# A row's sum of ReLU on one core: the first columns of the split row move to VectorE, and the last sum's two waits change places

## The chip, the cores and the metric

The kernel runs on one core of a Trainium2 chip. The metric is device time in microseconds (us). VectorE is DVE in the profile, ScalarE is ACT, SyncE is SP; DVEq and SPq are the sequencers of VectorE and SyncE. A *stamp* is a time read from the trace to the nanosecond, where the views of the profile round to hundredths of a microsecond. A *semaphore* is a counter that the program has an engine or a transfer raise (`then_inc`) and another wait for (`wait_op`, `wait_ge`). "Lands" means that the last of the sixteen semaphore updates arrives that the trace has for each load (in the kernel before, 154.913 to 155.398 for the load with rows 0 and 1). A sum is recorded as two instructions, the clamping and summing one and one that the trace calls the read of its *accumulator* (0.08 us on VectorE, 0.19 on ScalarE); the semaphore comes after that read (in the kernel before, VectorE's read of the first piece's sum ends at 157.721 and its semaphore comes at 157.732). "e1" to "e10" are the experiments.

## The reference, cut to what matters

```python
# x: (32, 512, 1024) float32, 64 MiB
relu_x = np.maximum(x, 0)
return np.sum(relu_x, axis=-1).astype(np.float32)
```

16,384 rows of 1024 columns, each clamped at zero and summed. On 128 partitions that is 128 rows a partition.

## The kernel before

The first 112 rows of every partition come in blocks of 16: mostly ScalarE clamps, VectorE sums. The last 16 come in loads of 8 and 4 rows, then the last four in a special cut. Of those four, rows 0, 1 and 3 are summed whole by ScalarE, VectorE and ScalarE. Row 2 is the **split row**: it is cut into four column ranges that arrive in four loads, so that little work is left behind the last byte. Each range is clamped and summed by itself. The last operation finds the other partial sums as extra columns behind its own data and adds them in (they are not negative, so the clamp doesn't change them).

```python
TAIL = [8, 4]
ACT_PIECE, END_PIECE = 340, 240     # first and last range of the split row
PIECES = [220, 224]                 # the two ranges between, which arrive last
...
def dve_row(ap, accum_out, loaded):          # VectorE: clamp and sum, one instruction
    i = nc.vector.tensor_scalar(out=ap, in0=ap, scalar1=0.0, scalar2=None,
                                op0=MAX, op1=ADD, accum_out=accum_out)
    if loaded is not None:
        i.wait_op(loaded, 16, "sem-ge")      # the wait is the instruction's own
    i.then_inc(sems.dve, 1)
...
loaded = load(flat[:, at : at + b], src[:, :b])          # rows 0, 1, first range of row 2
act_row(buf[:, c, :], res[:, m : m + 1], loaded)         # ScalarE: row 0
sums_act = n_act
act_row(flat[:, at + split : at + b], others[0], None)   # ScalarE: first range
piece_act = n_act
dve_row(buf[:, c + 1, :], res[:, m + 1 : m + 2], loaded) # VectorE: row 1
sums_dve = n_dve
loaded = load(flat[:, at + end : at + 4 * D], src[:, end:])  # last range of row 2, row 3
act_row(buf[:, c + 3, :], res[:, m + 3 : m + 4], loaded)     # ScalarE: row 3
dve_row(flat[:, at + end : at + 3 * D], others[1], loaded)   # VectorE: last range
... # loads of the two pieces; stores of the sums that are complete
for i in range(len(PIECES) - 1):
    dve_row(parts[i][:, :], others[2 + i], arrived[i])       # VectorE: first piece
nc.vector.wait_ge(sems.act, piece_act)
nc.vector.wait_ge(sems.dve, n_dve)
nc.vector.tensor_scalar(... last piece and the other sums ...,
    accum_out=res[:, NT - 2 : NT - 1],
).wait_op(arrived[-1], 16, "sem-ge").then_inc(sems.dve, 1)
n_dve += 1
store(NT - 2, 2, n_act, n_dve)     # SyncE waits for ScalarE, then for VectorE, and stores
```

Below, the load with the last range of row 2 and with row 3 is called the **second load**, the two pieces the **first** and the **last piece**.

Of the kernel before, what the change touches and what calls it, by code (L numbers as in the profile page):

```python
# [9 lines left out]
ROWS = 16  # L10
# [7 lines left out]


TAIL = [8, 4]  # L20
ACT_PIECE, END_PIECE = 340, 240
PIECES = [220, 224]

EARLY = 1

# [1 line left out]
def kernel(tc: tile.TileContext, x: bass.AP, out: bass.AP):  # L27
    nc = tc.nc
    sems = Semaphores(tc)

    tc.close()
    tc.compile()
    nc.cur_bb = nc.bb_map[tc.start_bb_name]
    body = nc.cur_bb.bb.instructions
    ends = list(body)
    body.clear()
    n_stores = relu_sum(nc, sems, x, out)
    body.extend(ends)


    nc.cur_bb = nc.bb_map[tc.start_bb_name + "_end"]
    nc.cur_bb.bb.instructions.clear()
    nums = sorted(s.num for s in (*sems.loads, sems.act, sems.dve))
    cleared = range(nums[0], nums[-1] + 1)
    assert len(cleared) == len(nums)
    nc.sync.sem_clear(cleared)
    nc.sync.wait_ge(sems.stored, 16 * n_stores).then_inc(sems.stored, -16 * n_stores)
    open_without_barrier(tc, EARLY)


class Semaphores:
    def __init__(self, tc: tile.TileContext):
        n = len(TWO) + len(TAIL) + 2 + len(PIECES)
        self.loads = [tc.alloc_semaphore(f"load{i}") for i in range(n)]
        self.act = tc.alloc_semaphore("act")
        self.dve = tc.alloc_semaphore("dve")
        self.stored = tc.alloc_semaphore("stored")


def relu_sum(nc, sems: Semaphores, x: bass.AP, out: bass.AP):  # L60
    x_flat = x.flatten_outer_dims()
    N, D = x_flat.shape
    NT = N // P
    NB = len(TWO)
    assert N == P * NT == P * ROWS * (NB + 1)
    assert sum(TAIL) == ROWS - 4 and ACT_PIECE + END_PIECE + sum(PIECES) == D

    bufs = [nc.alloc_sbuf_tensor(f"io{i}", [P, ROWS, D], F32) for i in range(NBUF)]
    res = nc.alloc_sbuf_tensor("res", [P, NT], F32)

    extra = len(PIECES) + 1
    parts = [
        nc.alloc_sbuf_tensor(f"piece{i}", [P, w + extra * (i + 1 == len(PIECES))], F32)
        for i, w in enumerate(PIECES)
    ]
# [21 lines left out]
    def load(dst, src, after=None):  # L97
        nonlocal n_load
        dma = nc.sync.dma_start(out=dst, in_=src)  # L99
        if after:  # L100
            dma.wait_op(sems.dve, after[1], "sem-ge")
        dma.then_inc(sems.loads[n_load], 16)
        n_load += 1
        return sems.loads[n_load - 1]
# [25 lines left out]
    def act_row(ap, accum_out, loaded):  # L130
        nonlocal n_act
        i = nc.scalar.activation(out=ap, in_=ap, func=RELU, accum_out=accum_out)  # L132
        if loaded is not None:
            i.wait_op(loaded, 16, "sem-ge")
        i.then_inc(sems.act, 1)
        n_act += 1

    def dve_row(ap, accum_out, loaded):
        nonlocal n_dve
        i = nc.vector.tensor_scalar(  # L140
            out=ap,
            in0=ap,
            scalar1=0.0,
            scalar2=None,
            op0=MAX,
            op1=ADD,
            accum_out=accum_out,
        )
        if loaded is not None:
            i.wait_op(loaded, 16, "sem-ge")  # L150
        i.then_inc(sems.dve, 1)
        n_dve += 1
# [40 lines left out]
    flat = buf[:, :, :].rearrange("p c d -> p (c d)")  # L193
    src = rows(m, 4).rearrange("p c d -> p (c d)")
    at = c * D
    split = 2 * D
    b = split + ACT_PIECE
    end = split + D - END_PIECE
    last, w = parts[-1], PIECES[-1]
    others = [last[:, w + i : w + i + 1] for i in range(extra)]  # L200
    loaded = load(flat[:, at : at + b], src[:, :b])
    act_row(buf[:, c, :], res[:, m : m + 1], loaded)
    sums_act = n_act
    act_row(flat[:, at + split : at + b], others[0], None)
    piece_act = n_act
    dve_row(buf[:, c + 1, :], res[:, m + 1 : m + 2], loaded)
    sums_dve = n_dve
    loaded = load(flat[:, at + end : at + 4 * D], src[:, end:])
    act_row(buf[:, c + 3, :], res[:, m + 3 : m + 4], loaded)
    dve_row(flat[:, at + end : at + 3 * D], others[1], loaded)  # L210
    arrived = []
# [9 lines left out]

    for i in range(len(PIECES) - 1):
        dve_row(parts[i][:, :], others[2 + i], arrived[i])
    nc.vector.wait_ge(sems.act, piece_act)
    nc.vector.wait_ge(sems.dve, n_dve)  # L225
    nc.vector.tensor_scalar(  # L226
        out=last[:, :],
        in0=last[:, :],
# [2 lines left out]
        op0=MAX,  # L231
        op1=ADD,
        accum_out=res[:, NT - 2 : NT - 1],
    ).wait_op(arrived[-1], 16, "sem-ge").then_inc(sems.dve, 1)
    n_dve += 1
    store(NT - 2, 2, n_act, n_dve)
    return n_store
# [49 lines left out]
```

## Time and profile before

| | before |
|---|---|
| median of three runs | 161.2 us (161.14 to 161.52) |
| span of the profiled run | 159.7 us |
| VectorE, ScalarE busy | 117.2 us (73%), 104.7 us (66%) |
| input moved | 67.11 MB at 421 GB/s, so 159.4 us |
| last piece lands (stamp) | 157.566 us |
| last store issued (stamp) | 158.306 us |

The table is read from its last rows. The input takes the whole span up to 157.57 (the packets take 98.0% of 16 engines' span by the page). What this change works on is the 0.74 us from there to the issue of the last store. From that issue to the end of the span are 1.426 us (stamps).

### The profile page before, as it was taken

What the parts mean: (1) busy time and instruction counts of PE and PEld (TensorE: products, weight loads), DVE (VectorE), ACT (ScalarE), POOL (GpSimd) and SP (SyncE); (2) the same over time, 40 slices, a digit from 0 to 9 for tenths busy, and PEclk for the clock granted to TensorE, in tenths of its full rate; (3) what the DMA queues carried; (4) which work ended last, traced back from release to release, by engine and by line L of the source; (5) the groups of instructions that cost most, each with busy time, mean ns of one, the idle gap of its engine ahead of it and who ended that gap; (6) DMA issues with size and microseconds to landing.
All of it is one profiled execution on the core that took longest, in us unless ns stands there. A gap on an engine that the chain in (4) does not pass through costs nothing.

```text
span 159.7 us, 120 instructions
## 1 busy us (share of the span) xinstructions
DVE 117.2 (73%) x41; ACT 104.7 (66%) x52; POOL 0.2 (0%) x4
## 2 busy tenths in 40 slices
DVE  0000000009999499994999999999999999999985
ACT  3000059990699708996099941999339992499996
POOL 0000000000000000000000000000000000000000
DMA  7996996996997999979979969969969969898993
GB/s 263 525 525 263 525 525 263 525 492 295 525 460 328 525 394 394 525 345 443 525 328 460 525 279 509 525 263 525 525 263 525 492 295 525 345 443 386 414 417 113
DMA packets 2304, 67.18 MB, mean 421 GB/s; under 512 B 640, under 2 KB 896, under 8 KB 1024
## 3 DMA queue, kind: packets, MB, share of 16 engines
q1 hardware_dynamic: 2304, 67.18, 98.0%
HBM read 67.11 MB, written 0.07 MB: 421 GB/s over the span
## 4 chain that ended last, share of the span: by engine, by line
DMA 44%; DVE 33%; ACT 17%; another core or an unknown queue 3%; SPq 1%; issue 0%; DVEq 0%
DMA io<-in_x_dram 44%; DVE res L125 32%; ACT io L117 17%; SPq L99 1%; DVE io L140 0%; DVE piece L226 0%; DVE piece L140 0%; DVEq L225 0%
## 5 line engine op out<-in xcount | busy, mean ns | idle before, releaser
L125 DVE TENSOR_REDUCE res<-io 128x8 f32<-128x8192 f32 (+2 forms) x9 | 101.1, 11287 | 40.0 <-ACT io L117 40.0
L117 ACT ACTIVATE io<-io 128x8192 f32<-128x8192 f32 (+2 forms) x9 | 81.7, 9110 | 47.7 <-DMA io<-in_x_dram 47.7
L132 ACT ACTIVATE io<-io 128x1024 f32<-128x1024 f32 (+1 forms) x21 | 21.3, 1017 | 5.7 <-DMA io<-in_x_dram 5.7
L140 DVE TENSOR_SCALAR_CACHE_REDUCE io<-io 128x1024 f32<-128x1024 f32 (+1 forms) x14 | 15.5, 1157 | 0.9 <-DMA io<-in_x_dram 0.9
L132 ACT ACTIVATION_READ_ACCUMULATOR io<-io 128x1 f32 x21 | 3.9, 187 | 0.0
L117 ACT ACT_TABLE_LOAD x1 | 1.3, 1283 | 0.1
L140 DVE DVE_READ_ACCUMULATOR io<-io 128x1 f32 x14 | 1.2, 82 | 0.0
L226 DVE TENSOR_SCALAR_CACHE_REDUCE piece<-piece 128x227 f32<-128x227 f32 x1 | 0.4, 390 | 0.2 <-DVE piece L140 0.2
L140 DVE TENSOR_SCALAR_CACHE_REDUCE piece<-piece 128x220 f32<-128x220 f32 x1 | 0.4, 378 | 0.0
L271 POOL MEMSET const-bfloat16-1.0<- 128x1 bf16 x1 | 0.1, 102 | 0.0
L271 POOL MEMSET const-uint8-127<- 128x1 uint8 x1 | 0.1, 102 | 0.0
L271 POOL MEMSET const-float32-0.0<- 128x1 f32 x1 | 0.1, 99 | 0.2 <-issue 0.2
L271 POOL MEMSET const-float32-1.0<- 128x1 f32 x1 | 0.1, 99 | 0.0
L140 DVE DVE_READ_ACCUMULATOR piece<-piece 128x1 f32 x1 | 0.1, 85 | 0.0
L226 DVE DVE_READ_ACCUMULATOR piece<-piece 128x1 f32 x1 | 0.1, 83 | 0.0
## 6 DMA issues: line engine op xcount, KB each, us to landing
io<-in_x_dram SPq DMA_DIRECT2D x1, 4096.0 KB, 21.6
io<-in_x_dram SPq DMA_DIRECT2D x1, 2048.0 KB, 26.1
io<-in_x_dram SPq DMA_DIRECT2D x1, 1194.0 KB, 28.5
io<-in_x_dram SPq DMA_DIRECT2D x1, 632.0 KB, 29.6
io<-in_x_dram SPq DMA_DIRECT2D x7, 26.9
piece<-in_x_dram SPq DMA_DIRECT2D x1, 112.0 KB, 29.2
piece<-in_x_dram SPq DMA_DIRECT2D x1, 110.0 KB, 29.4
out_dram<-res SPq DMA_DIRECT2D x1, 55.0 KB, 1.6
```

Of the source, the lines that this page charges most:

```text
L99: dma = nc.sync.dma_start(out=dst, in_=src)
L117: i = nc.scalar.activation(out=ap, in_=ap, func=RELU)
L125: nc.vector.tensor_reduce(out=res[:, m : m + n], in_=ap, axis=mybir.AxisListType.X, op=ADD).wait_op(sems.act, n_act, "sem-ge").then_inc(se ...
L132: i = nc.scalar.activation(out=ap, in_=ap, func=RELU, accum_out=accum_out)
L140: i = nc.vector.tensor_scalar(out=ap, in0=ap, scalar1=0.0, scalar2=None, op0=MAX, op1=ADD, accum_out=accum_out,)
L226: nc.vector.tensor_scalar(out=last[:, :], in0=last[:, :], scalar1=0.0, scalar2=None, op0=MAX, op1=ADD, accum_out=res[:, NT - 2 : NT - 1],) ...
L271: nc = _bacc.Bacc("TRN2", target_bir_lowering=False, num_devices=1)
```

## The change

Its intent: ScalarE is relieved of the first range, which VectorE sums in time in which it waits for the second load. The last operation then needs nothing of ScalarE. Its one remaining wait for other sums becomes its own, and the wait for its load, expected to be met earlier, stands ahead as an instruction. The cut is moved with it.

```diff
-ACT_PIECE, END_PIECE = 340, 240
-PIECES = [220, 224]
+START_PIECE, END_PIECE = 280, 260
+PIECES = [240, 244]
...
-    act_row(flat[:, at + split : at + b], others[0], None)
-    piece_act = n_act
     dve_row(buf[:, c + 1, :], res[:, m + 1 : m + 2], loaded)
     sums_dve = n_dve
+    dve_row(flat[:, at + split : at + b], others[0], None)
...
-    nc.vector.wait_ge(sems.act, piece_act)
-    nc.vector.wait_ge(sems.dve, n_dve)
+    nc.vector.wait_ge(arrived[-1], 16)
     nc.vector.tensor_scalar(
...
-    ).wait_op(arrived[-1], 16, "sem-ge").then_inc(sems.dve, 1)
+    ).wait_op(sems.dve, n_dve, "sem-ge").then_inc(sems.dve, 1)
```

More of the change, by code (lines that the diff above doesn't have):

```diff
@@ L65, in relu_sum @@
     assert N == P * NT == P * ROWS * (NB + 1)
-    assert sum(TAIL) == ROWS - 4 and ACT_PIECE + END_PIECE + sum(PIECES) == D
+    assert sum(TAIL) == ROWS - 4 and START_PIECE + END_PIECE + sum(PIECES) == D
     bufs = [nc.alloc_sbuf_tensor(f"io{i}", [P, ROWS, D], F32) for i in range(NBUF)]
@@ L196, in relu_sum @@
     split = 2 * D
-    b = split + ACT_PIECE
+    b = split + START_PIECE
     end = split + D - END_PIECE
```

## The prediction

> **What bounds the kernel now.** I read the page first, for the engine shares and the DMA row:
>
> ```profile
> DVE 117.2 (73%) x41; ACT 104.7 (66%) x52; POOL 0.2 (0%) x4
> ...
> HBM read 67.11 MB, written 0.07 MB: 421 GB/s over the span
> ```
>
> No compute engine is full. The transfers are: 67.11 MB at 421 GB/s is 159.4 us of a span of 159.7. The change moves no byte more or less, so the body of the kernel can't change. What is left is the end, where the input has landed and the last sums are still to be made and stored. So second I read the chain of waits, its last part in order of time (start, duration, what):
>
> ```profile
> 127.39 29.59 DMA io<-in_x_dram
> 156.98 0.02 issue
> 157.01 0.41 DVE io L140 x2
> 157.42 0.32 DVE piece L140 x2
> 157.73 0.03 issue
> 157.76 0.05 DVEq L225
> 157.81 0.07 issue
> 157.88 0.40 DVE piece L226 x2
> ```
>
> The end is set by VectorE: three sums after the load that lands at 156.98 (240, 220 and 224+3 columns), and between the second and the third a wait that is an instruction of its own (DVEq L225). Third, the timeline of the last 5 us (start, duration, engine, line, operation), to see which engines have room there:
>
> ```profile
> 155.42 1.22 DVE L140 TENSOR_SCALAR_CACHE_REDUCE io<-io 128x1024 f32<-128x1024 f32 x1 [0.51 <-DMA io<-in_x_dram]
> 156.38 0.19 ACT L132 ACTIVATION_READ_ACCUMULATOR io<-io 128x1 f32 x1
> 156.47 0.47 ACT L132 ACTIVATE io<-io 128x340 f32<-128x340 f32 x1
> 156.57 0.08 DVE L140 DVE_READ_ACCUMULATOR io<-io 128x1 f32 x1
> ...
> 157.00 1.06 ACT L132 ACTIVATE io<-io 128x1024 f32<-128x1024 f32 x1
> 157.01 0.40 DVE L140 TENSOR_SCALAR_CACHE_REDUCE io<-io 128x240 f32<-128x240 f32 x1 [0.36 <-DMA io<-in_x_dram]
> 157.33 0.08 DVE L140 DVE_READ_ACCUMULATOR io<-io 128x1 f32 x1
> 157.33 0.38 DVE L140 TENSOR_SCALAR_CACHE_REDUCE piece<-piece 128x220 f32<-128x220 f32 x1
> 157.64 0.09 DVE L140 DVE_READ_ACCUMULATOR piece<-piece 128x1 f32 x1
> 157.88 0.39 DVE L226 TENSOR_SCALAR_CACHE_REDUCE piece<-piece 128x227 f32<-128x227 f32 x1 [0.16 <-DVE piece L140]
> 157.97 0.19 ACT L132 ACTIVATION_READ_ACCUMULATOR io<-io 128x1 f32 x1
> 158.20 0.08 DVE L226 DVE_READ_ACCUMULATOR piece<-piece 128x1 f32 x1
> ```
>
> VectorE sits idle for 0.36 us before 157.01: that is where the added sum will go. It is idle again for 0.16 us before 157.88: that is the wait's cost. ScalarE's last sum ends at 157.97 + 0.19 = 158.16, VectorE's at 158.28. The last store needs both, so ScalarE is only 0.12 us behind: more than that the change can't gain by speeding VectorE alone. The last store is issued at 158.31 (stamp of the trace), takes 1.4 us to land (DMA issues of the page), and that ends the span.
>
> When do the four last loads land? Issue start plus issue-to-landing gives 126.89 + 28.5 = 155.39 (rows 0, 1 and the first 340 columns of row 2), 127.39 + 29.6 = 156.99 (the end of row 2 and row 3), 127.87 + 29.4 = 157.27 (220 columns), 128.37 + 29.2 = 157.57 (224 columns). Row 2 is the split row. The third sum at 157.88 therefore waits for no load: its data had been there for 0.31 us.
>
> [...] L225 is such a one, 50 ns busy on VectorE's sequencer, and from the second sum's semaphore at 157.73 to the third sum's start at 157.88 pass 0.15 us. Where an instruction carries the wait itself, as the 1024-column sum at 155.42 does, start follows the last landing update (stamp 155.398) by 0.02 us. [...] with a sum taken along, start to start is 1.15 us for 1024 columns and 0.32 us for 240, so 1.05 ns a column[...]; I cost columns at 1.05 ns. [...]
>
> **The change, part by part.**
>
> Loads. Columns of the split row go from 340 | 220 | 224 | 240 to 280 | 240 | 244 | 260. The first load shrinks by 60 columns (1194 to 1164 KB), the second grows by 20 (632 to 642), the pieces by 20 each (110 and 112 to 120 and 122). The sum is the same and so is the last landing, 157.57. Between the landings at 155.40 and 156.98, 632 KB took 1.58 us, that is 2.5 ns per KB. The first load lands 30 KB earlier, 0.07 us: 155.32. The second lands 20 KB earlier, 0.05 us: 156.93. The first piece 10 KB earlier: 157.25.
>
> ScalarE loses the 340-column sum, 0.47 + 0.19 us less some overlap. It lay between 156.47 and 157.04, and the row-3 sum behind it starts 0.02 us after its load. So this frees ScalarE but moves its end only with the load: 158.16 - 0.05 = 158.11. Off the path: worth nothing by itself.
>
> VectorE gains a 280-column sum. Start to start: 0.33 for 240 columns plus 40 x 1.05 ns = 0.37 us. It begins when the 1024-column sum gives way, 155.34 + 1.15 = 156.49, and is over at 156.86, before the load at 156.93. It fits into the idle time with 0.07 us to spare. Cost on the path: nothing.
>
> VectorE's sums after that load: 260 columns 0.35, 240 columns 0.33, from 156.95: the second gives way at 157.63, its accumulator read ends 0.085 us later and the semaphore comes at about 157.73. That is the same stamp as before: 0.05 us earlier start, 40 columns (0.04 us) more.
>
> The wait. Before: semaphore 157.73, sequencer wait, third sum at 157.88. After: the load's wait stands ahead as its own instruction and is met at 157.57, so it is done by about 157.57 + 0.02 + 0.05 = 157.64, and the sum can be in place by 157.71 (0.07 us from the end of the sequencer's wait to the start is what the old one took). The sum's own wait then fires 0.02 us after 157.73: start 157.75. **Saved: 0.13 us.** The last sum has 247 columns for 227: 0.02 us back.
>
> Sum at the end: 0.01 earlier semaphore or none, -0.13, +0.02: VectorE's last semaphore moves from 158.29 to about 158.18. ScalarE, at 158.11 to 158.12, stays just behind. The store is the same 1 KB. So the time falls by **about 0.1 us**, from 161.2 to 161.1, 0.07%.
>
> **Rivals.**
>
> *The wait is only exchanged.* If the separate wait on the load holds the sequencer so that the last sum is pushed late, part of the 0.13 us stays. For it: the margin above is only 0.02 to 0.04 us (157.71 against 157.75). Against it: the load lands 0.16 us before the other sum's semaphore. It would leave 161.15 to 161.2.
>
> *VectorE becomes late.* If the first load does not land 0.07 us earlier, the added sum runs from 156.57 to 156.94, just where the second load lands. Then the path grows by up to the added columns: 20 + 20 + 20 at 1.05 ns, 0.06 us, against 0.13 saved; net gain 0.05 us, still 161.15. A loss needs both rivals together, and then some 0.05 us: 161.25.
>
> *ScalarE becomes the bound.* Its end follows its load only. If VectorE gained more than 0.12 us, ScalarE's 158.16 would cap it. This caps the gain at 0.1 to 0.17 us; no larger one is to be had.
>
> *The transfers hide or undo it.* Bytes and number of loads are the same[...], so I give this little. The spread between executions is larger than anything here: the three before lie from 161.14 to 161.52.
>
> **Range and chances.** The working gives 161.1, rivals 161.05 to 161.25. The scatter of the runs before, 0.4 us upward and little downward, is wider than that: I take 160.85 to 161.4. Two per cent is 3.2 us; the whole stretch from the last landing to the end is only 159.7 - 157.57 = 2.1 us, of which 1.4 is the store. No mechanism reaches either bound of 2%, so within 2% has 0.98[...].
>
> **What would show it.** In the profile after: no sequencer wait between the second and the third sum, or one that ends by 157.65; idle time ahead of the last sum 0.02 to 0.05 us in place of 0.16; a 280-column sum on VectorE in front of the 260-column one, with under 0.1 us of idle time left between them; ScalarE's row-3 sum straight after its load; the last VectorE accumulator read ending near 158.17 in place of 158.28; a span of about 159.6. Wrong would make it: a 260-column sum that starts late because of the added sum, or a last sum that still begins 0.1 us or more after its neighbour's semaphore, or a landing of the last piece after 157.73.

One term of the forecast is an estimate that the new cuts of the row cost the transfers nothing in sum. That term was nought; what the sum came to is a semaphore 0.01 us earlier or none, 0.13 saved at the wait, 0.02 back for the longer last sum, so VectorE's last semaphore from 158.29 to about 158.18 and the time from 161.2 to about 161.1. The last sum must keep its wait for the other sums; every version here keeps that wait, so no run shows what happens without it.

## The result, and the profile after

161.07 us (six runs, 160.92 to 161.28) against 161.17 us for the kernel before (six runs, the first three among them). The ratio is 0.9988, 95% interval 0.9972 to 1.0003. A ratio is the mean time of one kernel's runs over that of the other's of the same rounds, so it is not quite the ratio of the medians quoted here. The verdict is "same": within 2%, and by this comparison not even clear of no change. The experiments below return to that.

The last part of the chain of waits of the changed kernel (start, duration, what):

```profile
126.91 28.43 DMA io<-in_x_dram
155.34 0.02 issue
155.37 2.02 DVE io L140 x6
157.39 0.33 DVE piece L140 x2
157.72 0.02 issue
157.74 0.42 DVE piece L224 x2
```

No DVEq is left in it: from the second sum's semaphore (157.72) to the last sum there are 0.02 us in place of 0.15. The timeline of the same stretch (start, duration, engine, line, operation, and in brackets the idle time before it with what ended it):

```profile
156.51 0.44 DVE L140 TENSOR_SCALAR_CACHE_REDUCE io<-io 128x280 f32<-128x280 f32 x1
...
156.88 0.08 DVE L140 DVE_READ_ACCUMULATOR io<-io 128x1 f32 x1
156.95 1.06 ACT L132 ACTIVATE io<-io 128x1024 f32<-128x1024 f32 x1 [0.44 <-DMA io<-in_x_dram]
156.95 0.42 DVE L140 TENSOR_SCALAR_CACHE_REDUCE io<-io 128x260 f32<-128x260 f32 x1
157.30 0.08 DVE L140 DVE_READ_ACCUMULATOR io<-io 128x1 f32 x1
157.30 0.40 DVE L140 TENSOR_SCALAR_CACHE_REDUCE piece<-piece 128x240 f32<-128x240 f32 x1
157.63 0.08 DVE L140 DVE_READ_ACCUMULATOR piece<-piece 128x1 f32 x1
157.74 0.41 DVE L224 TENSOR_SCALAR_CACHE_REDUCE piece<-piece 128x247 f32<-128x247 f32 x1
157.92 0.19 ACT L132 ACTIVATION_READ_ACCUMULATOR io<-io 128x1 f32 x1
158.08 0.08 DVE L224 DVE_READ_ACCUMULATOR piece<-piece 128x1 f32 x1
```

The added 280-column sum gives way at 156.88 (where its accumulator read begins), the 260-column sum begins at 156.95, at the same time as ScalarE's row 3. ScalarE had been idle for 0.44 us and was started by the load. So the load started both, and VectorE had 0.08 us to spare. The chain says something else: it draws one unbroken piece of VectorE from 155.37 on. That comes from the accumulator read, whose recorded end (stamp 156.958) lies a little behind the load's landing (156.930), though the next sum starts before that end. Which of the two readings holds is tested below.

### The profile page after: what moved, and what is told of

Same layout as the page of the kernel before. It is cut to its first block, busy times and chain, and to the rows that moved or that the text cites. A ratio compares the mean times of both kernels' runs of the same rounds, so it can differ in the third digit from the quotient of the medians.

```text
span 159.6 us, 120 instructions
## 1 busy us (share of the span) xinstructions
DVE 117.6 (74%) x43; ACT 104.2 (65%) x50; POOL 0.2 (0%) x4
## 3 DMA queue, kind: packets, MB, share of 16 engines
HBM read 67.11 MB, written 0.07 MB: 421 GB/s over the span
## 4 chain that ended last, share of the span: by engine, by line
DMA 43%; DVE 34%; ACT 17%; another core or an unknown queue 3%; SPq 1%; issue 0%
DMA io<-in_x_dram 43%; DVE res L125 32%; ACT io L117 17%; DVE io L140 1%; SPq L99 1%; DVE piece L224 0%; DVE piece L140 0%
## 5 line engine op out<-in xcount | busy, mean ns | idle before, releaser
L132 ACT ACTIVATE io<-io 128x1024 f32<-128x1024 f32 x20 | 20.9, 1045 | 6.0 <-DMA io<-in_x_dram 6.0
L140 DVE TENSOR_SCALAR_CACHE_REDUCE io<-io 128x1024 f32<-128x1024 f32 (+2 forms) x15 | 15.8, 1110 | 0.5 <-DMA io<-in_x_dram 0.4
L132 ACT ACTIVATION_READ_ACCUMULATOR io<-io 128x1 f32 x20 | 3.8, 188 | 0.0
```

The lines of the kernel that those rows point to most:

```text
L132: i = nc.scalar.activation(out=ap, in_=ap, func=RELU, accum_out=accum_out)
```

## The experiments

Landings move from run to run, by up to 0.29 us against the predicted ones in e3 and 0.7 in e4, more than what is to be found. So the stamps are first taken relative to two landings of the same run. The table has all runs with a profile; columns: from the second load's landing to the last piece's; from the second sum's semaphore to the start of the last sum; then the last semaphore of VectorE, that of ScalarE and the issue of the last store, all from the second load's landing; the store from the last landing; the median of the timed runs and the ratio to the kernel before in the same rounds.

| run | 2nd load to last | semaphore to last sum | VectorE | ScalarE | store | store from last | us | ratio |
|---|---|---|---|---|---|---|---|---|
| before | 0.584 | 0.149 | 1.308 | 1.182 | 1.324 | 0.740 | 161.17 | |
| before, again | 0.537 | 0.147 | 1.306 | 1.181 | 1.323 | 0.786 | 161.21 | 1.0006 |
| changed | 0.674 | 0.023 | 1.242 | 1.181 | 1.258 | 0.584 | 161.07 | 0.9988 |
| changed, again | 0.668 | 0.023 | 1.245 | 1.180 | 1.262 | 0.594 | 160.99 | 0.9992 |
| changed, third | 0.666 | 0.024 | 1.252 | 1.181 | 1.269 | 0.603 | 161.00 | 0.9991 |
| e1, waits alone | 0.544 | 0.024 | 1.179 | 1.182 | 1.245 | 0.701 | 161.12 | 0.9996 |
| e2, columns alone | 0.680 | 0.120 | 1.348 | 1.181 | 1.365 | 0.685 | 161.24 | 1.0004 |
| e3, three sums | 0.634 | 0.025 | 1.263 | 1.182 | 1.280 | 0.646 | 161.16 | 1.0005 |
| e4, nine waits more | 0.649 | 0.198 | 1.415 | 1.182 | 1.432 | 0.783 | 161.26 | 1.0012 |
| e5, sum on ScalarE | 0.686 | 0.025 | 1.266 | 1.181 | 1.282 | 0.596 | 161.04 | 0.9996 |
| e6, 300/240 | 0.680 | 0.024 | 1.273 | 1.180 | 1.290 | 0.610 | 161.11 | 0.9997 |
| e9, 215/299 | 0.681 | 0.069 | 1.288 | 1.181 | 1.304 | 0.623 | 161.09 | 0.9994 |

All ten runs gave the right result.

One thing more is needed to compare runs, because the table's landings may themselves have moved. The load of four rows ahead of the special cut (the 4 of `TAIL`) is the same in every version, and so is the number of bytes behind it. Counted from its landing (stamps of the same traces):

| run | first load | second load | last piece | store |
|---|---|---|---|---|
| before | 2.873 | 4.457 | 5.041 | 5.781 |
| before, again | 2.873 | 4.500 | 5.037 | 5.823 |
| e1, waits alone | 2.884 | 4.481 | 5.025 | 5.726 |
| changed | 2.800 | 4.388 | 5.062 | 5.646 |
| changed, again | 2.796 | 4.403 | 5.071 | 5.665 |
| changed, third | 2.801 | 4.400 | 5.066 | 5.669 |
| e2, columns alone | 2.790 | 4.402 | 5.082 | 5.767 |
| e3, three sums | 2.796 | 4.429 | 5.063 | 5.709 |
| e4, nine waits more | 2.785 | 4.433 | 5.082 | 5.865 |
| e5, sum on ScalarE | 2.794 | 4.390 | 5.076 | 5.672 |
| e6, 300/240 | 2.862 | 4.465 | 5.145 | 5.755 |
| e9, 215/299 | 2.792 | 4.401 | 5.082 | 5.705 |

With the new cut the first load lands 0.078 us earlier and the second 0.082 (means of the first three rows and of the three of the changed kernel), but the last piece 0.032 later; the ranges of the two groups don't overlap. The store of the changed kernel comes 0.142 earlier than that of the kernel before (mean of two).

**e1: the waits alone.** The theory at this point: the exchange of the waits is the whole gain. The rival: the move of columns pays. The kernel before, with only this:

```diff
     nc.vector.wait_ge(sems.act, piece_act)
-    nc.vector.wait_ge(sems.dve, n_dve)
+    nc.vector.wait_ge(arrived[-1], 16)
...
-    ).wait_op(arrived[-1], 16, "sem-ge")
+    ).wait_op(sems.dve, n_dve, "sem-ge")
```

> Kernel before with the wait exchanged alone (columns stay 340 | 220 | 224 | 240, ScalarE still sums the 340). Theory (the exchange of the waits is the whole gain): the last VectorE sum starts 0.02 us after the semaphore of the sum before it, at about 157.75 in place of 157.88; last VectorE semaphore near 158.16 (before 158.29, changed kernel 158.17); ScalarE's end stays at 158.16, level with it. Time as the changed kernel, about 0.1 us under before. Rival (the move of columns to VectorE is what pays): little or nothing is gained, last sum still 0.1 us or more after its neighbour's semaphore or stopped by ScalarE.

The timeline of this run:

```profile
157.87 0.39 DVE L226 TENSOR_SCALAR_CACHE_REDUCE piece<-piece 128x227 f32<-128x227 f32 x1
158.09 0.19 ACT L132 ACTIVATION_READ_ACCUMULATOR io<-io 128x1 f32 x1
158.19 0.08 DVE L226 DVE_READ_ACCUMULATOR piece<-piece 128x1 f32 x1
```

and its chain:

```profile
126.98 28.52 DMA io<-in_x_dram
155.50 0.02 issue
155.53 2.75 ACT io L132 x6
```

VectorE gains 0.128 us (1.307 before, the mean of its two runs, to 1.179), and the last sum follows its semaphore by 0.024 us. But the store gains only 0.079. ScalarE's read ends at 158.28, later than VectorE's by 5 ns, and the chain has changed engine: it is ScalarE, L132, to the end. The store has the same two kinds of wait as the sum had. ScalarE's is an instruction ahead of it (SPq L109, 17 ns busy), and from that semaphore to the issue pass 0.063 us, against 0.016 from VectorE's, which is the store's own. So ScalarE caps the end at 1.245 us after the second load. By the trace, the exchange is the larger part but not the whole; the theory that it is everything falls. The time (0.9996, 0.9983 to 1.0008) can't tell.

**e2: the columns alone.** The changed kernel with the old order of waits:

```diff
-    nc.vector.wait_ge(arrived[-1], 16)
+    nc.vector.wait_ge(sems.dve, n_dve)
...
-    ).wait_op(sems.dve, n_dve, "sem-ge")
+    ).wait_op(arrived[-1], 16, "sem-ge")
```

> Changed kernel with the old waits: the load is the last sum's own wait, the wait for the other sums is an instruction ahead of it. Theory: the move of columns alone gains nothing; 0.15 us between the second sum's semaphore (157.72) and the last sum's start (157.87), last VectorE semaphore about 158.30, as before (158.29) or 0.01 later; time within 0.03 us of before. Rival (columns pay): time 0.05 us or more under before.

Counted from the second load, VectorE's end is 0.041 us later than before. Sixty columns more at 1.05 ns are 0.063 (start to start, 220 columns took 0.302 us in the kernel before and 280 took 0.365 in the changed one; stamps); of that 0.028 comes back, because the wait in front of the last sum has one condition instead of two (21 ns busy, L223, instead of 50, L225, and 0.120 from semaphore to start instead of 0.148). Against it stands that the second load lands earlier relative to the last landing: 0.680 us ahead, against 0.584, 0.537 and 0.544 in the three runs with the old cut. So from the last landing the store comes 0.078 sooner than before (0.685 against 0.763, the mean of two). But the last landing itself is later with the new cut: counted from the four-row load, the store gains 0.035 (5.767 against 5.802). One run is behind this figure, and the two runs before differ by 0.042, so it is small or nothing. The time is 1.0004, no gain, as expected.

**e3: is VectorE the path all along, as the chain draws it, or does the second load start it?** The 280 columns are summed in three instructions:

```diff
-    dve_row(flat[:, at + split : at + b], others[0], None)
+    cuts = [at + split, at + split + 94, at + split + 188, at + b]
+    for lo, hi, o in zip(cuts, cuts[1:], (others[0], others[-2], others[-1])):
+        dve_row(flat[:, lo:hi], o, None)
```

> Changed kernel with the 280 columns summed in three instructions of some 93 on VectorE (two extra partial sums, read by the last one). Each extra instruction has 0.075 us of fixed cost: 0.15 us more work ahead of the 260-column sum. Theory (the load that lands at 156.93 sets the start of the 260-column sum, with 0.08 us of VectorE to spare): that sum starts at about 157.03, 0.07 us later, last semaphore about 158.25. Rival (VectorE is the path without a break from 155.37 on, as the chain of waits names it): the full 0.15 us, start 157.10, last semaphore about 158.33.

The 0.075 can be had, as an estimate, from the kernel before: 240 columns took 0.328 us from start to start (stamps), less 240 at 1.05 ns, which leaves 0.076.

The timeline of this run (the accumulator reads between are left out):

```profile
156.76 0.25 DVE L140 TENSOR_SCALAR_CACHE_REDUCE io<-io 128x94 f32<-128x94 f32 x1
...
156.93 0.24 DVE L140 TENSOR_SCALAR_CACHE_REDUCE io<-io 128x94 f32<-128x94 f32 x1
...
157.10 0.24 DVE L140 TENSOR_SCALAR_CACHE_REDUCE io<-io 128x92 f32<-128x92 f32 x1
157.25 1.06 ACT L132 ACTIVATE io<-io 128x1024 f32<-128x1024 f32 x1 [0.48 <-DMA io<-in_x_dram]
...
157.27 0.42 DVE L140 TENSOR_SCALAR_CACHE_REDUCE io<-io 128x260 f32<-128x260 f32 x1
```

Now VectorE starts 0.02 us behind ScalarE, which the same load released. The three took 0.510 us from the first's start to that of the 260-column sum, 0.145 more than the one (0.365), so 0.073 for each extra instruction. The 260-column sum began 0.046 us after the second load's landing instead of 0.024, so 0.022 of the 0.145 came through. The size expected was 0.07; in this run the second load came 1.633 us after the first, against 1.588 in the changed kernel, which gave VectorE 0.045 us more to spare. With that the sum is right: 0.145 less 0.079 less 0.045. The chain's reading would have had 0.145; it falls. A chain that goes through an engine's own previous instruction is not proof that the engine had no slack.

**e4: what does a wait instruction cost in that place?** Nine more waits ahead of the last sum:

```diff
     nc.vector.wait_ge(arrived[-1], 16)
+    nc.vector.wait_ge(sems.dve, n_dve)
+    for earlier in sems.loads[:8]:
+        nc.vector.wait_ge(earlier, 16)
```

> Changed kernel with nine waits more on VectorE between the second and the last sum: one for the other sums, eight for loads that landed long ago. Theory (a wait instruction behind the second sum stands on the path): each instruction that is left of them costs 0.05 us or more, so 0.3 to 0.7 us later end and time, the last store with it. Rival (the end is set by ScalarE or by a transfer): the time stays within 0.1 us of the changed kernel.

The 0.05 agrees with the 50 ns that L225 is busy in the kernel before.

The line of the waits (count, then busy ns min/median/max):

```profile
L226 DVEq EVENT_SEMAPHORE  x5: 50/50/153, 158.0 to 158.5; - x5
```

The ten waits were built as five instructions of two conditions, in another order than written. The first four start about 0.10 us apart, twice their 50 ns. Three were over before the second sum's semaphore (stamp 158.453): those cost nothing. The fourth held that semaphore's condition: it is recorded from 158.336 to 158.489, 153 ns, so in this record the time spent waiting is inside the span. One more came behind it: from the semaphore to the last sum 0.198 us, against 0.023. The store comes 0.17 us later than in the changed kernel, the time is 1.0012. The size expected, 0.3 to 0.7, was a miss: it assumed that all of them would stand behind the semaphore. The first began when the second sum did (158.036 and 158.037), so four of them started while it ran. The direction holds. In this run only the two wait instructions that were not over when the last event came stood on the path, for 0.175 us; the three that were over did not.

**e5: does it matter which engine sums the first range?** The changed kernel with the sum given back:

```diff
     sums_act = n_act
+    act_row(flat[:, at + split : at + b], others[0], None)
+    piece_act = n_act
...
-    dve_row(flat[:, at + split : at + b], others[0], None)
...
+    nc.vector.wait_ge(sems.act, piece_act)
     nc.vector.wait_ge(arrived[-1], 16)
```

> Changed kernel with the 280-column sum given back to ScalarE, cut and exchanged wait kept. All counted from the landing of the second load (row 3 and end of row 2), because the landings themselves move by up to 0.3 us from run to run. Theory (which engine sums the first columns is of no account; the cut counts, because ScalarE's and VectorE's ends hang on that landing, and the wait counts): the last store is issued 1.26 us after it, as in the changed kernel (1.258; before 1.324; wait alone 1.245; columns alone 1.365), 0.58 after the last landing. Rival (taking the sum off ScalarE matters): ScalarE's row-3 sum starts late, store later by 0.05 us or more.

ScalarE's row 3 began 0.023 us after its load (0.023 in the kernel before, 0.022 in the changed one); the rival falls. The store is 1.282 from the second load, 0.02 later than expected, but 0.596 from the last landing, where the three runs of the changed kernel have 0.584 to 0.603, and 5.672 from the four-row load, where they have 5.646 to 5.669. Most of the 0.02 is the first piece: it landed 0.366 us after the second load (0.342 in the changed kernel), and VectorE's second sum had to wait for it. The columns before it were done at 157.226 (stamp), it started at 157.243:

```profile
157.23 0.08 DVE L140 DVE_READ_ACCUMULATOR io<-io 128x1 f32 x1
157.24 0.40 DVE L140 TENSOR_SCALAR_CACHE_REDUCE piece<-piece 128x240 f32<-128x240 f32 x1
```

So the move from ScalarE to VectorE by itself is worth nothing that these stamps show. What it does is to free the last operation of a condition, and with the load's wait ahead that condition did not stand on the path either: here, with it, 0.025 us from semaphore to last sum, against 0.023 without.

**e6: twenty columns from behind the second load to the front.**

```diff
-START_PIECE, END_PIECE = 280, 260
+START_PIECE, END_PIECE = 300, 240
```

> Changed kernel with 300 | 240 | 244 | 240: twenty columns more in front, twenty fewer behind the second load. Theory (VectorE has about 0.08 us to spare ahead of that load, and ScalarE caps the end at 1.245 us after it): VectorE's last semaphore 0.02 us earlier against that landing, 1.22; the store 1.245 after it, held by ScalarE, 0.01 gained; not to be seen in the time. Rival (VectorE is the path from the first load on): no gain at all.

No gain: 0.610 from the last landing. The rival's outcome, but not for its reason. The timeline of this run:

```profile
157.03 0.40 DVE L140 TENSOR_SCALAR_CACHE_REDUCE io<-io 128x240 f32<-128x240 f32 x1
157.36 0.08 DVE L140 DVE_READ_ACCUMULATOR io<-io 128x1 f32 x1
157.41 0.40 DVE L140 TENSOR_SCALAR_CACHE_REDUCE piece<-piece 128x240 f32<-128x240 f32 x1
```

Between 157.36 and 157.41 VectorE waits: the shorter sum is done before the first piece has landed (stamp 157.383). The path has gone from VectorE's columns to a landing. Counted from the four-row load all four landings of this run are 0.06 to 0.08 later than in the changed kernel, and the store 0.095 (5.755 against 5.660, the mean of three). Whether the cut does that or this one run, isn't shown.

**e7, e8, e10: the changed kernel twice more, the kernel before once more.** No edit.

> The changed kernel once more, for the scatter. Theory: store 1.26 us after the second load's landing, second load to last landing 0.63 to 0.68 us (0.58 and 0.54 in the two runs of the old cut); time 0.05 to 0.15 us under before. Rival (the gain is scatter): ratio at or above 1.

> The kernel before against itself, as a control of what a ratio of these rounds is worth. Expected: ratio 1 within 0.001; store 1.32 us after the second load's landing, 0.54 to 0.59 from there to the last landing, store 0.74 after the last landing. If the ratio is off by as much as the changed kernel's 0.0012, the time does not settle the gain and only the stamps do.

> The changed kernel a third time, beside the new cut. Expected as before: store 1.26 after the second load's landing and 0.58 to 0.60 after the last one; ratio to the kernel before 0.999.

The stamps repeat: within 0.011 us counted from the second load, within 0.05 from the last landing. The control of the kernel before against itself gave 1.0006 (0.9993 to 1.0019), so one ratio of such rounds is uncertain by about as much as the effect. Three comparisons of the changed kernel gave 0.9988, 0.9992 and 0.9991, each with an upper end just above 1. All 16 timed runs of the changed kernel have a mean of 161.03 us, all 40 of the kernel before 161.19: 0.15 us apart, with a standard error of 0.03 from the scatter within each set. (Those 40 include rounds in which other kernels stood beside it.)

**e9: a cut meant to beat both.**

```diff
-START_PIECE, END_PIECE = 280, 260
-PIECES = [240, 244]
+START_PIECE, END_PIECE = 280, 230
+PIECES = [215, 299]
```

> A version meant to beat both: changed kernel cut 280 | 215 | 299 | 230. Theory (three limits meet: the second load's landing with ScalarE's row behind it, the first piece's landing ahead of VectorE's second sum, VectorE's columns): 30 columns moved into the last pieces let the second load land some 0.04 us earlier against the last landing, and the first piece, smaller, lands before VectorE asks for it. Second load to last landing 0.70 to 0.73 (0.67 with the changed cut), store 1.26 after the second load, so 0.53 to 0.56 after the last landing (changed kernel 0.584 and 0.594). In time 0.05 us at most, not clear of scatter. Rival (the changed cut is already the best): 0.58 or more.

The 0.04 is an estimate that can be had from the prediction's: 30 columns are 15 KB, at 2.5 ns a KB.

A miss: 0.623, and 5.705 from the four-row load. The second load did not come earlier against the last landing (0.681), and a further limit appeared:

```profile
157.47 0.08 DVE L140 DVE_READ_ACCUMULATOR piece<-piece 128x1 f32 x1
157.64 0.47 DVE L224 TENSOR_SCALAR_CACHE_REDUCE piece<-piece 128x302 f32<-128x302 f32 x1
```

The second sum is done early, its semaphore is there at 157.568 (stamp). The last sum starts 0.069 us after it and 0.120 us after the last landing (157.517): now the load is the late event, and its wait is the instruction ahead. This is the prediction's first rival, brought about by the cut. In the changed kernel the same wait ended at 157.653 (stamp) and the sum began at 157.742. At the 0.07 us that the old wait took from its end to the sum, there were 0.02 us to spare.

So no version here beats the changed kernel. Around it lie four limits within about 0.02 us each, the first two counted from the second load: VectorE's columns (store at 1.26), ScalarE's row (1.245), the first piece's landing (157.272 in the changed kernel, where the sum that needs it starts at 157.303) and the last piece's wait (the 0.02 us to spare).

## Why the prediction was right

- **The end, not the body.** Right: 67.11 MB at 421 GB/s in both pages, and all that differs lies behind 155 us.
- **The landings.** First load 155.32 predicted, 155.342 measured; second 156.93 and 156.930; first piece 157.25 and 157.272; last 157.57 and 157.604. The match of the second is partly luck: see its lead, below.
- **The added sum fits.** It gives way at 156.875 (predicted 156.86), 0.08 us ahead (0.07). e3 shows that this slack is real.
- **The wait.** The load's wait ended at 157.653 (157.64), the last sum began at 157.742 (157.75) after a semaphore at 157.719 (157.73). The 0.13 us are there: 0.125 in the changed kernel, 0.124 in e1 (against 0.148 before, the mean of two).
- **The sum.** VectorE's last semaphore 158.172 (158.18), ScalarE's 158.111 (158.11), the time 161.07 (161.1). This close agreement is partly luck of one profile: in other runs of the same cut the landings lie up to 0.29 us from the predicted ones (e3), in e4 0.7.
- **ScalarE as the next bound.** The mechanism was right and shown by e1; the size was off. The prediction allowed 0.12 us of gain before ScalarE caps it, by comparing the two semaphores. The store's wait for ScalarE costs 0.047 us more than that for VectorE (0.063 against 0.016), so the exchange alone realises 0.079.
- **The second load's lead.** Here two terms were mis-sized. The prediction had the second load 0.05 us earlier, from 20 KB at 2.5 ns a KB, and the last landing unmoved, from equal bytes (and from the estimate). Counted from the four-row load, the second load came 0.082 earlier and the last piece 0.032 later. So the lead of the one over the other grew from 0.555 (mean of three runs of the old cut) to 0.669 (mean of the three runs of the changed kernel), 0.11. From the second load to the store there are 1.324 and 1.263 (means), 0.06 gained, as the prediction's terms behind that load give (0.11 less 0.05); with the 0.08 before it that makes 0.14. The pooled times say 0.15. Both are more than the 0.1 predicted, because of the second load, and within the 0.1 to 0.17 that the prediction allowed. The bytes behind the second load grew from 222 to 242 KB, 9%, its lead by 20%: bytes alone don't explain it. Why the landings move so, the runs don't show.

Both parts are needed, and for a reason that the prediction only half had. The exchange takes VectorE's end back (1.307 to 1.179 us after the second load, e1) until ScalarE's end caps it (store at 1.245). The new cut brings the second load 0.082 us earlier, and ScalarE's end with it, which stays 1.180 to 1.182 behind that load in all twelve profiles; that lifts the cap. In stamps from the four-row load: 0.08 for the waits alone, 0.04 for the columns alone, 0.14 for both; the two runs before differ by 0.04 and the three of the changed kernel by 0.02, and the first two figures rest on one run each.

## What to carry to other kernels

As far as these runs go: where an operation needs two waits, and one of them stands ahead of it as an instruction, let the operation carry the one that is met last. Here the instruction ahead cost 0.10 to 0.12 us on VectorE when its event was the late one (0.05 at SyncE's store), and nothing that shows when it was met 0.12 us before the other (changed kernel, 0.023 us from semaphore to sum); at 0.05 before it still cost 0.05 (e9). Before counting such a gain, work out when the next engine ends and which of the final store's waits it stands on. Where the effect is smaller than the scatter of the landings, compare stamps relative to a landing of the same run, one that the change can't move, and run the kernel before against itself to see what a ratio is worth.
